# Odd-layer parameters gathered into one DRAM array, and the second half's norm placed between projections

## The chip, the cores and the metric

The kernel runs on one core of a Trainium2 chip. A core has five engines: TensorE (PE; its weight loads are shown apart as PEld), VectorE (DVE), ScalarE (ACT), GpSimd (POOL) and SyncE (SP). Each runs its own instructions strictly in order and waits on semaphores for the others. SP computes nothing here; it issues nearly all loads and stores between DRAM and the on-chip memory (SBUF), which 16 DMA engines then carry out from queues. The metric is the device time of one execution in microseconds.

## The reference, cut to what matters

A trunk of two layers works on x, 1024 tokens by 1024 features, in float32. Layer 0 (even) has an S5 state-space model and stick-breaking attention side by side; layer 1 (odd) has RWKV-7 and Mamba-2 side by side. Each mixer is followed by a mixture of experts (32 experts, two per token). Every sub-layer is normed and modulated by shift, scale and gate vectors that a matrix ada_w makes of the conditioning vector c:

```python
def odd_mixer(h, w_in, w_out, rw_mu, rw_w0, rw_w2, rw_a0, rw_a2, rw_g2, rw_k_k, rw_k_a,
              rw_r_k, rw_ln_w, rw_ln_b, m2_conv_w, m2_conv_b, m2_dt_bias, m2_a_log, m2_d, m2_norm_w):
    proj = h @ w_in
    y_c = rwkv7_mixer(proj[..., :RW_IN], rw_mu, rw_w0, rw_w2, rw_a0, rw_a2, rw_g2,
                      rw_k_k, rw_k_a, rw_r_k, rw_ln_w, rw_ln_b)
    y_d = mamba2_mixer(proj[..., RW_IN:], m2_conv_w, m2_conv_b, m2_dt_bias, m2_a_log, m2_d, m2_norm_w)
    return jnp.concatenate([y_c, y_d], axis=-1) @ w_out
```

The small vectors and matrices after w_out are the parameters of the odd layer that the change is about: vectors of 512 to 1792 values, a convolution of 4 x 1024, two matrices of 64 x 512 and one of 128 x 512, and an eight-column slice of w_in. What they hold doesn't depend on x.

## The kernel before

Tokens are worked on in eight tiles of 128; the odd layer's first projections run over the first four (the first half), and the second four are normed beside them and put away in DRAM. A float32 product is three matmuls on a high and a low part of each operand: mm3 (L240 to L242). The parts come from split (L136 to L139), ScalarE copying the high part, VectorE subtracting to get the low one, for weights (wh, wl) and for the normed activations (hTh, hTl).

ada (L142) makes the modulation vectors: four pieces of ada_w, 1 MB each, are loaded through SP (wload, L77), VectorE multiplies each by c in eight steps (L160 once, L167 seven times) into adacc, TensorE sums over partitions (L179) and VectorE adds a bias (L180). The first two vectors, scale and shift of the even mixer, need eight pieces and stay in SBUF; later ones are made between other work and stored to mod_d in DRAM (L187), value by value. In the even layer a loop over eight loads of its input weights (L2047) runs the projections. Inside the experts' routing a table tab_d goes to DRAM value by value, too (L1202); u_d, an S5 operand, goes in pieces of 256 bytes (L262).

The odd layer (odd, L1829) begins with norm_S over tiles 0 to 3, then odd_setup, then norm_S over tiles 4 to 7, and only then starts the generator project(0, 13) and runs it dry with poke(1e9) (L1886). poke(us) advances the generator in self.bg until it has reported so many microseconds of work. Norming a tile first completes the experts of layer 0 for it: get loads the residual cx and the two expert outputs cy (L990, L994), VectorE merges them (L1008), for some tiles with POOL (L1005), the result is stored to xm_d (L1854), normed (L131, L201), transposed by TensorE (L106) and modulated (L223 on ScalarE, L225 on VectorE). A projection's result goes through a token shift (L1402) or through m_conv (L1370), a convolution whose part on ScalarE is L1382.

odd_setup (L1216) loads the parameters through SP into a tile each: seven vectors and rk as columns of 128 (col, L111; each value is a piece of four bytes, since neighbours in DRAM lie in different partitions), cw in four (L1260), wdt (L1262), wa2 in two (L1264, L1265), g2 (L1267), dtb and al (L1270, L1272), md (row, L117), and the layer-norm vectors in four (L1308). VectorE then scales some (L1276).

What is written here is not the final order on an engine: the framework's scheduler simulates the program by its own costs and gives each engine an order, in which an instruction may be put ahead of others that stand earlier in the code. In the trace before, the transposes of tiles 4 to 7 already stand between projection matmuls.

Of the kernel before, what the change touches and what calls it, by code (L numbers as in the profile page):

```python
# [23 lines left out]
KD = D // 128  # L24
# [12 lines left out]
class Core:  # L37
# [1177 lines left out]

    def odd_setup(self, one, tag):  # L1216
# [41 lines left out]
        R["cw"] = one.tile([128, 4, 8], FT, name="cw")  # L1258
        for j in range(4):
            nc.sync.dma_start(R["cw"][:, j, :], a["m2_conv_w"][0, j].rearrange("(k p) -> p k", p=128))  # L1260
        R["wdt"] = one.tile([128, KD, 8], FT, name="wdt")
        nc.sync.dma_start(R["wdt"], a["odd_w_in"][0][:, 3328:3336].rearrange("(k p) n -> p k n", p=128))  # L1262
        R["wa2"] = one.tile([128, 512], FT, name="wa2")
        nc.sync.dma_start(R["wa2"][0:64, :], a["rw_w2"][0])  # L1264
        nc.sync.dma_start(R["wa2"][64:128, :], a["rw_a2"][0])  # L1265
        R["g2"] = one.tile([128, 512], FT, name="g2w")
        nc.sync.dma_start(R["g2"], a["rw_g2"][0])  # L1267
# [5 lines left out]
        R["md"] = self.row(one, a["m2_d"][0], "md", 8, nc.sync)  # L1273
# [29 lines left out]

        for nm in ("rw_ln_w", "rw_ln_b"):
            t = R[nm] = one.tile([128, 4, 64], FT, name=nm)
            src = a[nm][0]
            for r in range(2):
                nc.sync.dma_start(t[64 * r:64 * r + 64], bass.AP(tensor=src.tensor, offset=src.offset + 64 * r,  # L1308
                                                                   ap=[[0, 64], [128, 4], [1, 64]]))
# [519 lines left out]
    def odd(self, get, y_d, o, after):  # L1829
# [3 lines left out]
        with ctx:  # L1833
# [17 lines left out]
            with tc.tile_pool(name="nr1", bufs=1) as np_:  # L1851
# [16 lines left out]
            pos = [0]  # L1868

            def project(n0, n1):  # L1870
                for n in range(n0, n1):
                    pos[0] = n
                    h, (_, do, c) = plan[n]
                    load(n + 1)
                    src = box.pop(n)
                    for z in range(2):
                        w = [pj.tile([128, KD, 128], FR, name=x, bufs=2) for x in ("wh", "wl")]
                        self.split(*w, src[:, :, 128 * z:128 * z + 128])
                        yield from do(h, c + z, w, hs, R, pj)
                    pos[0] = n + 1  # L1880
                    if n in (5, 20):
                        yield from self.m_dt(h, hs, R, pj)
# [96 lines left out]
    def even(self, x_src):  # L1979
# [9 lines left out]
        with self.banks("pse", b=4, a=1, d=1, e=2):  # L1989
# [16 lines left out]
            with tc.tile_pool(name="hT", bufs=1, side="right") as hp, tc.tile_pool(name="wsp", bufs=1, side="right") as wp:  # L2006
# [40 lines left out]
                for n in range(8):  # L2047
# [137 lines left out]
```

## Time and profile before

| | us |
|---|---|
| median of 3 runs | 3070.61 |
| lowest, highest | 3070.59, 3075.35 |
| profiled execution | 3069.93 |
| its span (first to last instruction) | 3068.1 |
| TensorE busy | 2656.4 |
| VectorE busy | 1792.6 |
| ScalarE busy | 1120.7 |
| GpSimd busy | 831.2 |

The mean granted TensorE clock was 0.902 of full speed. Busy times are sums over the whole span; they overlap. An engine that is idle matters only where another waits for it in turn, so a table like this tells which engine is busy, and the timelines below tell where it isn't.

### The profile page before, as it was taken

What the parts mean: (1) busy time and instruction counts of PE and PEld (TensorE: products, weight loads), DVE (VectorE), ACT (ScalarE), POOL (GpSimd) and SP (SyncE); (2) the same over time, 40 slices, a digit from 0 to 9 for tenths busy, and PEclk for the clock granted to TensorE, in tenths of its full rate; (3) what the DMA queues carried; (4) which work ended last, traced back from release to release, by engine and by line L of the source; (5) the groups of instructions that cost most, each with busy time, mean ns of one, the idle gap of its engine ahead of it and who ended that gap; (6) DMA issues with size and microseconds to landing.
All of it is one profiled execution on the core that took longest, in us unless ns stands there. A gap on an engine that the chain in (4) does not pass through costs nothing. (4 is left out here: it accounts for less than half of the span.)

```text
span 3068.1 us, 39923 instructions
## 1 busy us (share of the span) xinstructions
PE 2656.4 (87%) x14357; PEld 1854.7 (60%) x14357; DVE 1792.6 (58%) x3211; ACT 1120.7 (37%) x1777; POOL 831.2 (27%) x1157
## 2 busy tenths in 40 slices
PE   4987688989699999995799999999978799998991
PEld 4776466647444466662677777777877444566660
DVE  7546999655633477664734555646547434556664
ACT  4311456432232345552433323323233223345451
POOL 5260755324211031101301533354105111111101
PEclk9998689989799999997898978886988799999996
DMA  8746220223588899997745322244443689999995
GB/s 279 178 124 198 63 59 15 90 68 105 211 338 324 351 368 407 376 389 256 260 138 176 110 77 78 67 121 103 107 125 119 242 348 365 369 362 396 388 385 239
DMA packets 345018, 672.82 MB, mean 219 GB/s; under 512 B 118591, under 2 KB 259935, under 8 KB 293104
## 3 DMA queue, kind: packets, MB, share of 16 engines
q1 hardware_dynamic: 272960, 611.23, 54.7%
q10 hardware_dynamic: 56752, 25.41, 3.0%
q0 software_dynamic: 15104, 33.58, 3.0%
q8 instruction: 115, 1.88, 0.3%
q14 instruction: 87, 0.71, 0.1%
HBM read 611.31 MB, written 79.79 MB: 225 GB/s over the span
## 5 line engine op out<-in xcount | busy, mean ns | idle before, releaser
L139 DVE TENSOR_TENSOR wlo<-w,whi 128x1024 fp32r<-128x1024 f32 x384 | 451.4, 1220 | 114.0 <-ACT whi L138 112.3
L138 ACT ACTIVATE whi<-w 128x1024 fp32r<-128x1024 f32 x384 | 390.5, 1054 | 237.1 <-PE ps_g L839 69.9
L240 PE MATMUL ps_b<-hTh,wh 128*128 128x512 f32 x608 | 259.3, 428 | 28.2 <-ACT cc L1382 12.5
L241 PE MATMUL ps_b<-hTl,wh 128*128 128x512 f32 x608 | 255.2, 420 | 0.0
L242 PE MATMUL ps_b<-hTh,wl 128*128 128x512 f32 x608 | 254.8, 419 | 0.0
L788 POOL DMA_INDIRECT xg<-h_d,tok x56 | 80.6, 1440 | 641.6 <-PE ps_t L106 617.1
L847 DVE TENSOR_TENSOR hs<-hs,ps_u 128x512 f32<-128x512 f32 x48 | 32.9, 685 | 263.3 <-PE ps_u L917 212.4
L794 POOL DMA_INDIRECT ye_d<-y,tab x48 | 71.9, 1497 | 421.8 <-DVE y L856 328.4
L167 DVE SCALAR_TENSOR_TENSOR adacc<-w,cs,adacc 128x256 f32<-128x256 f32 x329 | 161.1, 507 | 5.2
L139 DVE TENSOR_TENSOR wl<-w,wh 128x1024 fp32r<-128x1024 f32 x84 | 104.0, 1253 | 97.3 <-ACT wh L138 88.1
L240 PEld LDWEIGHTS ps_b<-hTh,wh 128*128 128x128 f32 x608 | 124.8, 206 | 55.9 <-ACT cc L1382 13.3
L846 ACT ACTIVATE hs<-ps_g 128x512 f32<-128x512 f32 x48 | 28.7, 598 | 325.0 <-PE ps_g L917 244.8
L313 DVE TENSOR_TENSOR_SCAN sP<-keep,sP,sbz 128x256 f32<-128x256 f32 (+1 forms) x160 | 132.9, 874 | 21.7 <-POOL keep L307 10.5
L917 PE MATMUL ps_g<-w,xh 128*64 128x512 f32 x512 | 143.5, 598 | 0.0
L133 POOL TENSOR_TENSOR rs<-rm,nhalf 128x1 f32<-128x1 f32 (+2 forms) x56 | 49.9, 892 | 344.9 <-DVE rm L131 293.2
L138 ACT ACTIVATE wh<-w 128x1024 fp32r<-128x1024 f32 x84 | 86.3, 1053 | 150.5 <-PE ps_b L241 132.4
L241 PEld LDWEIGHTS ps_b<-hTl,wh 128*128 128x128 f32 x608 | 124.7, 205 | 27.2 <-DVE hTl L139 0.3
L242 PEld LDWEIGHTS ps_b<-hTh,wl 128*128 128x128 f32 x608 | 123.9, 204 | 28.3 <-issue 0.4
L917 PE MATMUL ps_u<-w,xh 128*64 128x512 f32 x512 | 137.6, 595 | 0.0
L315 POOL TENSOR_TENSOR sw<-sw,sP 128x512 f32<-128x512 f32 (+1 forms) x80 | 101.1, 1265 | 132.6 <-DVE sP L313 57.3
L926 PE MATMUL ps_y<-w,hh 128*64 128x512 f32 x512 | 122.0, 598 | 2.2 <-ACT hh L921 2.2
L1699 POOL TENSOR_TENSOR T<-N,X 128x60 f32<-128x60 f32 (+24 forms) x248 | 87.1, 351 | 125.2 <-DMA N<-n_d 93.3
(709 smaller groups left out, 6177.9 us busy)
## 6 DMA issues: line engine op xcount, KB each, us to landing
w<-in_moe_w_gate_dram SPq DMA_DIRECT2D x128, 1024.0 KB, 14.7
w<-in_moe_w_up_dram SPq DMA_DIRECT2D x128, 1024.0 KB, 14.8
w<-in_moe_w_down_dram SPq DMA_DIRECT2D x128, 1024.0 KB, 13.4
w<-in_ada_w_dram SPq DMA_DIRECT2D x48, 1024.0 KB, 5.8
w<-in_odd_w_in_dram SPq DMA_DIRECT2D x26, 1024.0 KB, 5.7
cy<-ye_d SPq DMA_DIRECT2D x16, 1024.0 KB, 10.8
cx<-xm_d SPq DMA_DIRECT2D x29, 512.0 KB, 7.5
w<-in_even_w_in_dram SPq DMA_DIRECT2D x8, 1024.0 KB, 8.5
```

The lines of the kernel that those rows point to most:

```text
L138: self.nc.scalar.activation(hi, x, AF.Copy)
L139: self.nc.vector.tensor_tensor(lo, x, hi.bitcast(FT), op=OP.subtract)
L167: eng.scalar_tensor_tensor(acc, wk, ck, acc, op0=OP.mult, op1=OP.add)
L240: nc.tensor.matmul(p, a[0], b[0], start=first, stop=False)
L241: nc.tensor.matmul(p, a[0], b[1], start=False, stop=False)
L242: nc.tensor.matmul(p, a[1], b[0], start=False, stop=last)
L313: v.tensor_tensor_scan(P[:, r, 0:n][:, ::-1], keep[:, r, 0:n][:, ::-1], zero.to_broadcast([128, n]), P[:, r, n:n + 1], op0=OP.mult, op1=OP ...
L315: g.tensor_tensor(w[:, :, 0:n], w[:, :, 0:n], P[:, :, 1:n + 1], op=OP.mult)
L788: nc.gpsimd.indirect_dma_start(out=xg, out_offset=None, in_=h_d[:], in_offset=bass.IndirectOffsetOnAxis(ap=tokc, axis=0), bounds_check=T - ...
L917: nc.tensor.matmul(ps[z][r], x[:, 4 * h + k, r], w[z][h][:, k, :], start=(h == 0 and k == 0), stop=(h == 1 and k == 3))
L926: nc.tensor.matmul(py[n][r], ht[:, f, r], w[2][f // 2][:, f % 2, two[n]], start=(f == 0), stop=(f == 3))
L1699: g.tensor_tensor(o, N[:, 0:j, j:j + 1].to_broadcast([128, j, w]), X[:, j:j + 1, c:8].to_broadcast([128, j, w]), op=OP.mult)
```

## The change

Three edits. First, a new function pack, called in the even layer's loop at its seventh weight load, copies 15 parameters of the odd layer from DRAM to DRAM, into one array pk_d of 128 rows by 1686 values, laid out as SBUF wants them; odd_setup then loads pk_d by one transfer into the tile pk and uses slices of it (dtb and al are still loaded by themselves). Second, norm_S of tiles 4 to 7 is called in two pairs, each after poke(18) of the projection generator, which is created before. Third, the two steps on al (Exp and the sign) stand right behind odd_setup.

```diff
+    def pack(self):
+        nc, a = self.nc, self.a
+        self.pk, parts, c = {}, [], 0
+        col = lambda src: src.rearrange("(k p) -> p k", p=128)
+        for nm, n in (("rw_w0", 4), ("rw_a0", 4), ("rw_k_k", 4), ("rw_k_a", 4), ("m2_conv_b", 8), ("m2_norm_w", 4), ("rw_mu", 14)):
+            parts.append((nm, n, [(slice(0, 128), slice(0, n), col(a[nm][0]))]))
+        parts.append(("rk", 4, [(slice(0, 128), slice(0, 4), col(a["rw_r_k"][0].rearrange("h n -> (h n)")))]))
+        parts.append(("cw", 32, [(slice(0, 128), slice(8 * j, 8 * j + 8), col(a["m2_conv_w"][0, j])) for j in range(4)]))
+        wdt = a["odd_w_in"][0][:, 3328:3336].rearrange("(k p) n -> p k n", p=128)
+        parts.append(("wdt", 64, [(slice(0, 128), slice(8 * k, 8 * k + 8), wdt[:, k]) for k in range(KD)]))
+        parts.append(("wa2", 512, [(slice(0, 64), slice(0, 512), a["rw_w2"][0]), (slice(64, 128), slice(0, 512), a["rw_a2"][0])]))
+        parts.append(("g2", 512, [(slice(0, 128), slice(0, 512), a["rw_g2"][0])]))
+        md = a["m2_d"][0]
+        parts.append(("md", 8, [(slice(0, 128), slice(0, 8), bass.AP(tensor=md.tensor, offset=md.offset, ap=[[0, 128], [1, 8]]))]))
+        for nm in ("rw_ln_w", "rw_ln_b"):
+            src = a[nm][0]
+            parts.append((nm, 256, [(slice(64 * r, 64 * r + 64), slice(64 * h, 64 * h + 64),
+                                     bass.AP(tensor=src.tensor, offset=src.offset + 128 * h + 64 * r, ap=[[0, 64], [1, 64]]))
+                                    for r in range(2) for h in range(4)]))
+        self.pk_n = sum(n for _, n, _ in parts)
+        self.pk_d = self.dram.tile([128, self.pk_n], FT, name="pk_d")
+        for nm, n, pieces in parts:
+            self.pk[nm] = c, n
+            for rows, cols, src in pieces:
+                nc.sync.dma_start(self.pk_d[rows, c + cols.start:c + cols.stop], src)
+            c += n
...
-        for nm, n in (("rw_w0", 4), ("rw_a0", 4), ("rw_k_k", 4), ("rw_k_a", 4),
-                      ("m2_conv_b", 8), ("m2_norm_w", 4), ("rw_mu", 14)):
-            R[nm] = self.col(one, a[nm][0], nm, n, nc.sync)
-        R["rk"] = self.col(one, a["rw_r_k"][0].rearrange("h n -> (h n)"), "rkc", 4, nc.sync)
+        pk = one.tile([128, self.pk_n], FT, name="pk")
+        nc.sync.dma_start(pk, self.pk_d[:])
+        for nm, (c, n) in self.pk.items():
+            R[nm] = pk[:, c:c + n]
...
-        for j in range(4):
-            nc.sync.dma_start(R["cw"][:, j, :], a["m2_conv_w"][0, j].rearrange("(k p) -> p k", p=128))
...
-        nc.sync.dma_start(R["g2"], a["rw_g2"][0])
...
-                for h, d in enumerate((hs, ht)):
-                    if h == 1:
-                        R = self.odd_setup(one, "a")
-                    self.norm_S(getx, self.mod["scale1", 1], self.mod["shift1", 1], *d, np_, "tk", range(4 * h, 4 * h + 4))
+                mod = self.mod["scale1", 1], self.mod["shift1", 1]
+                self.norm_S(getx, *mod, *hs, np_, "tk", range(4))
+                R = self.odd_setup(one, "a")
+                nc.scalar.activation(R["al"], R["al"], AF.Exp)
+                nc.vector.tensor_scalar(R["al"], R["al"], -1.0, None, op0=OP.mult)
...
+                self.bg = [project(0, 13)]
+
+                for t in (4, 6):
+                    self.poke(18)
+                    self.norm_S(getx, *mod, *ht, np_, "tk", range(t, t + 2), 128 * (t - 4))
...
-            nc.scalar.activation(R["al"], R["al"], AF.Exp)
-            nc.vector.tensor_scalar(R["al"], R["al"], -1.0, None, op0=OP.mult)
-            self.turn_tag = "t"
-            self.bg = [project(0, 13)]
             self.poke(1e9)
...
+                    if n == 6:
+                        self.pack()
```

Where the new transfers come to stand is the scheduler's doing. On SP at the very start of the program, before (xt is a tile of x, w a piece of a weight matrix; xN counts equal neighbours):

```order
L2013 DMA xt<-in_x_dram 128x1024 x4
L77 DMA w<-in_ada_w_dram 128x8x256 x4
L2013 DMA xt<-in_x_dram 128x1024 x2
L77 DMA w<-in_ada_w_dram 128x8x256
L2013 DMA xt<-in_x_dram 128x1024
L77 DMA w<-in_ada_w_dram 128x8x256
```

And the same place in the changed kernel:

```order
L2030 DMA xt<-in_x_dram 128x1024 x4
L77 DMA w<-in_ada_w_dram 128x8x256 x4
L1241 DMA pk_d<-in_rw_w_dram 128x4x1
L1241 DMA pk_d<-in_rw_a_dram 128x4x1
L1241 DMA pk_d<-in_rw_k_k_dram 128x4x1
L1241 DMA pk_d<-in_rw_k_a_dram 128x4x1
L2030 DMA xt<-in_x_dram 128x1024
L1241 DMA pk_d<-in_m_conv_b_dram 128x8x1
L1241 DMA pk_d<-in_m_norm_w_dram 128x4x1
L1241 DMA pk_d<-in_rw_mu_dram 128x14x1
L1241 DMA pk_d<-in_rw_r_k_dram 128x4x1
L1241 DMA pk_d<-in_m_conv_w_dram 128x8x1 x2
```

Behind these rows come another xt, the last two transfers of conv_w and one of wdt, and then the fifth piece of ada_w. So all transfers with single values in them have moved between the fourth and the fifth piece; the rest of the 40 follow among the pieces five to eight and the first input weights of the even layer.

On SP at the odd layer's start, before, from its second weight load on:

```order
L1264 DMA wa_11386<-in_rw_w_dram 64x512
L1854 DMA xm_d<-cx 128x1024
L1265 DMA wa_11386<-in_rw_a_dram 64x512
L1267 DMA g2w<-in_rw_g_dram 128x512
L1270 DMA dtb<-in_m_dt_bias_dram 8x1
L1272 DMA al<-in_m_a_log_dram 8x1
L117 DMA md<-in_m_d_dram 128x8
L1308 DMA rw_ln_w<-in_rw_ln_w_dram 64x4x64 x2
L1854 DMA xm_d<-cx 128x1024
L1308 DMA rw_ln_b<-in_rw_ln_b_dram 64x4x64 x2
L994 DMA cy<-ye_d 128x2048 x2
L77 DMA w<-in_odd_w_in_dram 128x8x256
```

And in the changed kernel:

```order
L77 DMA w<-in_odd_w_in_dram 128x8x256
L1279 DMA pk<-pk_d 128x1686
L1292 DMA dtb<-in_m_dt_bias_dram 8x1
L1294 DMA al<-in_m_a_log_dram 8x1
L77 DMA w<-in_odd_w_in_dram 128x8x256
L1868 DMA xm_d<-cx 128x1024 x3
L994 DMA cy<-ye_d 128x2048 x2
L1868 DMA xm_d<-cx 128x1024
L77 DMA w<-in_odd_w_in_dram 128x8x256
```

The cy loads now stand behind one parameter load, a second weight load and three stores of x, where before all the single loads stood ahead of them.

On TensorE, the place where transposes of tiles 4 to 7 first stand between the projections' matmuls, before (ps_t and ps_k are the transposes' accumulators, ps_b the projection's):

```order
L240 MATMUL ps_b<-hTh,wh 128x512
L106 MATMUL ps_t<-ident,cy 128x128
L106 MATMUL ps_k<-ident,cy 128x128 x2
L241 MATMUL ps_b<-hTl,wh 128x512
L242 MATMUL ps_b<-hTh,wl 128x512
L240 MATMUL ps_b<-hTh,wh 128x512
L106 MATMUL ps_t<-ident,cy 128x128 x3
L106 MATMUL ps_k<-ident,cy 128x128 x6
```

And after:

```order
L106 MATMUL ps_t<-ident,cy 128x128 x4
L106 MATMUL ps_k<-ident,cy 128x128 x8
```

The first pair's transposes come about six groups of three matmuls later and stand in one bunch of twelve; four more of that pair follow behind further projection matmuls.

## Rows read from the trace of the kernel before

**Rows 1.** The page: span; each engine's busy time; a group of instructions (busy, mean ns).
```profile
span 3068.1 us, 39923 instructions
...
PE 2656.4 (87%) x14357; PEld 1854.7 (60%) x14357; DVE 1792.6 (58%) x3211; ACT 1120.7 (37%) x1777; POOL 831.2 (27%) x1157
...
L167 DVE SCALAR_TENSOR_TENSOR adacc<-w,cs,adacc 128x256 f32<-128x256 f32 x329 | 161.1, 507 | 5.2
```

**Rows 2.** Windows: us, each engine's busy time, granted clock, DMA share, GB/s.
```profile
0.00:20.00 20.00, 4.20 (x16) 3.00 (x16) 6.86 (x20) 8.26 (x14) 12.57 (x13) 1.00 0.95 292
...
15.00:20.00 5.00, 3.51 (x14) 2.71 (x14) 4.82 (x9) 2.39 (x4) 4.90 (x4) 1.00 1.10 372
```

**Rows 3.** Timeline of SP's queue at the start: start, duration, line, transfer, count.
```profile
5.62 8.47 SPq L77 DMA_DIRECT2D w<-in_ada_w_dram  x4
...
20.83 0.38 SPq L77 DMA_DIRECT2D w<-in_ada_w_dram  x1
```

**Rows 4.** Timeline of DVE: first step of ada pieces five, seven, eight; the shift.
```profile
28.58 0.34 DVE L160 TENSOR_SCALAR adacc<-w,cs 128x256 f32<-128x256 f32 x1
...
39.66 1.17 DVE L160 TENSOR_SCALAR adacc<-w,cs 128x256 f32<-128x256 f32 x1
...
44.21 0.35 DVE L160 TENSOR_SCALAR adacc<-w,cs 128x256 f32<-128x256 f32 x1
...
50.86 0.17 DVE L180 TENSOR_TENSOR shift<-ps_e,adac 128x8 f32<-128x8 f32 x1
```

**Rows 5.** Timeline of PE: the first projection matmul [idle before, its releaser].
```profile
60.40 1.22 PE L240 MATMUL ps_b<-hTh,wh 128*128 128x512 f32 x2 [9.58 <-ACT hTh L138]
```

**Rows 6.** Timeline of DVE at the odd layer's start.
```profile
1452.40 0.18 DVE L1276 TENSOR_SCALAR cw<-cw 128x32 f32<-128x32 f32 x1 [1.76 <-DMA cw<-in_m_conv_w_dram]
...
1457.05 0.43 DVE L1276 TENSOR_SCALAR g2w<-g2w 128x512 f32<-128x512 f32 x1 [2.69 <-DMA g2w<-in_rw_g_dram]
...
1472.30 1.29 DVE L1008 SCALAR_TENSOR_TENSOR cx<-cy,gates,cx 128x1024 f32<-128x1024 f32 x1 [7.10 <-issue]
```

**Rows 7.** Timeline of SP's queue at the odd layer's start.
```profile
1428.61 7.21 SPq L111 DMA_DIRECT2D rw_w<-in_rw_w_dram  x1
...
1445.40 1.00 SPq L1854 DMA_DIRECT2D xm_d<-cx  x1
...
1458.43 1.04 SPq L994 DMA_DIRECT2D cy<-ye_d  x2
```

**Rows 8.** Timeline of PE there: first projection, and the third block of them.
```profile
1461.40 1.20 PE L240 MATMUL ps_b<-hTh,wh 128*128 128x512 f32 x2
...
1484.60 0.80 PE L240 MATMUL ps_b<-hTh,wh 128*128 128x512 f32 x1 [10.80 <-ACT cc L1382]
```

**Rows 9.** Waits of PE, 1460 to 1560: total us, times, longest us.
```profile
PE ps_b L240 <- ACT cc L1382: 12.5, 2, 10.8
PE ps_t L106 <- DVE acc L1402: 4.6, 1, 4.6
PE ps_k L106 <- ACT hm L223: 1.3, 1, 1.3
```

**Rows 10.** DMA view, 1442 to 1452 us: all packets, while small parameters load.
```profile
DMA packets 10741, 0.67 MB, mean 67 GB/s; under 512 B 10533, under 2 KB 10612, under 8 KB 10740
```

**Rows 11.** Line L187 (store of mod_d, eight times): issue to landing.
```profile
DMA to landing us min/median/max: 12.0/12.2/12.5
```

**Rows 12.** Window during the fifth such store.
```profile
286.00:297.00 11.00, 3.40 (x14) 2.25 (x14) 3.68 (x14) 1.02 (x1) 4.03 (x6) 0.68 0.48 23
```

**Rows 13.** Timeline of DVE behind it.
```profile
301.47 0.35 DVE L160 TENSOR_SCALAR adacc<-w,cs 128x256 f32<-128x256 f32 x1 [11.58 <-DMA w<-in_ada_w_dram]
```

**Rows 14.** Line L1202 (store of tab_d): issue to landing.
```profile
DMA to landing us min/median/max: 36.2/37.3/38.5
```

**Rows 15.** DMA view, 1107 to 1116 us: packets of the queue with that store.
```profile
q10 hardware_dynamic: 2290, 0.01, 16.2%
```

**Rows 16.** Line L262 (store of u_d, 256-byte pieces): issue to landing.
```profile
DMA to landing us min/median/max: 3.0/3.1/11.4
```

More of the change, by code (lines that the diff above doesn't have):

```diff
@@ L1249, in odd_setup @@
         v.tensor_copy(hbk[:].rearrange("p h k -> p (h k)"), ph[0:8])
-        for nm, n in (("rw_w0", 4), ("rw_a0", 4), ("rw_k_k", 4), ("rw_k_a", 4),
-                      ("m2_conv_b", 8), ("m2_norm_w", 4), ("rw_mu", 14)):
-            R[nm] = self.col(one, a[nm][0], nm, n, nc.sync)
-        R["rk"] = self.col(one, a["rw_r_k"][0].rearrange("h n -> (h n)"), "rkc", 4, nc.sync)
+        pk = one.tile([128, self.pk_n], FT, name="pk")
+        nc.sync.dma_start(pk, self.pk_d[:])
+        for nm, (c, n) in self.pk.items():
+            R[nm] = pk[:, c:c + n]
+        R["cw"] = R["cw"].rearrange("p (j k) -> p j k", j=4)
+        R["wdt"] = R["wdt"].rearrange("p (k n) -> p k n", k=KD)
+        for nm in ("rw_ln_w", "rw_ln_b"):
+            R[nm] = R[nm].rearrange("p (h d) -> p h d", h=4)
         R["nkk"] = one.tile([128, 4], FT, name="nkk")
@@ L1257, in odd_setup @@
         v.tensor_scalar(R["omu"], R["rw_mu"], -1.0, 1.0, op0=OP.mult, op1=OP.add)
-        R["cw"] = one.tile([128, 4, 8], FT, name="cw")
-        for j in range(4):
-            nc.sync.dma_start(R["cw"][:, j, :], a["m2_conv_w"][0, j].rearrange("(k p) -> p k", p=128))
[L1261 to L1266, printed above, removed]
-        nc.sync.dma_start(R["g2"], a["rw_g2"][0])
         R["dtb"] = one.tile([8, 1], FT, name="dtb")
@@ L1272, in odd_setup @@
         nc.sync.dma_start(R["al"], a["m2_a_log"][0].rearrange("(h o) -> h o", o=1))
-        R["md"] = self.row(one, a["m2_d"][0], "md", 8, nc.sync)
         for x in ("rw_w0", "rw_a0", "rw_k_a", "m2_conv_b", "cw", "g2"):
@@ L1302, in odd_setup @@
         v.tensor_scalar(bd[:, 0:1], R["odd32"], -1.0, 1.0, op0=OP.mult, op1=OP.add)
[L1304 to L1309, printed above, removed]
         R["n_d"] = self.dram.tile([8, 32, 1024], FT, name="n_d")
@@ L1860, in odd, with project @@
                 load(0)
-                for h, d in enumerate((hs, ht)):
-                    if h == 1:
-                        R = self.odd_setup(one, "a")
-                    self.norm_S(getx, self.mod["scale1", 1], self.mod["shift1", 1], *d, np_, "tk", range(4 * h, 4 * h + 4))
+                mod = self.mod["scale1", 1], self.mod["shift1", 1]
[3 more added lines that the diff above has]
+                nc.vector.tensor_scalar(R["al"], R["al"], -1.0, None, op0=OP.mult)
+                pos = [0]
+                def project(n0, n1):
+                    for n in range(n0, n1):
+                        pos[0] = n
+                        h, (_, do, c) = plan[n]
+                        load(n + 1)
+                        src = box.pop(n)
+                        for z in range(2):
+                            w = [pj.tile([128, KD, 128], FR, name=x, bufs=2) for x in ("wh", "wl")]
+                            self.split(*w, src[:, :, 128 * z:128 * z + 128])
+                            yield from do(h, c + z, w, hs, R, pj)
+                        pos[0] = n + 1
+                        if n in (5, 20):
+                            yield from self.m_dt(h, hs, R, pj)
+                self.turn_tag = "t"
+                self.bg = [project(0, 13)]
+                for t in (4, 6):
+                    self.poke(18)
+                    self.norm_S(getx, *mod, *ht, np_, "tk", range(t, t + 2), 128 * (t - 4))
                 h_d = self.dram.tile([2, 128, KD * 512], FT, name="h_d")
@@ L1867, in odd @@
                     nc.scalar.dma_start(h_d[z], ht[z][:].rearrange("p k t -> p (k t)").bitcast(FT))
[L1868 to L1882, printed above, removed]
-            nc.scalar.activation(R["al"], R["al"], AF.Exp)
-            nc.vector.tensor_scalar(R["al"], R["al"], -1.0, None, op0=OP.mult)
-            self.turn_tag = "t"
-            self.bg = [project(0, 13)]
             self.poke(1e9)
```

## The prediction

> **What bounds the kernel now.** The page comes first: the span is 3068.1 us and TensorE is busy for 2656.4 us of it, VectorE for 1792.6 [rows 1]. The profiled execution took 3069.93 us, 1.83 over its span, and lies 0.68 under the median of the runs shown; the sum below is made against 3069.93. An average of 87% says that TensorE sets the pace in most stages, not in which it waits. So I looked at the two places that the change touches, the start (the gather) and the first projections of the odd layer, by windows, then by each engine's timeline.
>
> At the start the core waits for loads. In the first 20 us the DMA engines are 95% busy at 292 GB/s and TensorE works 4.20 us [rows 2]. SP has put four pieces of ada_w into its queue by 14.1 us, behind four x tiles; the fifth piece follows at 20.83 [rows 3]. VectorE multiplies each piece as it comes: the fifth from 28.58 us, the seventh and eighth from 39.66 and 44.21, so 4.55 us a piece, and the finished shift stands at 50.86 [rows 4]. The first matmul of a projection comes at 60.40 us, after 9.58 us of waiting for the normed tile [rows 5]. What makes the fifth piece late makes this late, and no TensorE work lies beside it.
>
> In the odd layer VectorE waits 1.76 us for cw and 2.69 us for g2w, and later stands 7.10 us before the merge of expert outputs at 1472.30 [rows 6]. The view names "issue"; SP's queue shows the true releaser: the cy loads of that merge are issued at 1458.43 only, behind the parameter loads, the first of them at 1428.61 [rows 7]. Instructions of one engine run in order, so the convolution steps queued behind that merge wait too, and TensorE, whose projections begin at 1461.40, stands 10.80 us until 1484.60 for them [rows 8]. Smaller waits follow up to 1560: 1.7 more of the 12.5 on the convolution, 4.6 for a shift step and 1.3 for a modulation, 18.4 in all with the 10.80 [rows 9].
>
> **The gather's cost.** pack() issues 40 transfers from DRAM to DRAM on SP. 78 columns of 128 values go element by element, 9984 pieces of 4 bytes. Wdt adds 1024 pieces of 32 bytes and md 128, the layer-norm vectors 1024 of 256 bytes, and three matrices 0.5 MB in rows of 2 KB. The code calls it in the even layer's loop, but the scheduler puts the first 13 transfers between the fourth and the fifth load of ada_w, so all 9984 elements stand in the queue ahead of the piece that VectorE needs at 28.58.
>
> No such transfer is in the trace; bounds come from its neighbours.
> - Lowest: the same parameters loaded into SBUF, 10533 small packets within a window of 10 us [rows 10]. So C = 10 us.
> - Highest: the store of mod_d writes 1024 four-byte elements to DRAM and lands after 12.2 us [rows 11]; in 11 us of it the loads run at 23 GB/s only, and VectorE then waits 11.58 us for a piece of ada_w [rows 12, 13]. That is 11 us / 1024 = 10.7 ns each, C = 9984 x 10.7 ns = 107 us.
> - Between: the store of tab_d, 4096 such elements, lands after 37.3 us [rows 14], but beside weight loads; its last 2290 passed in at most 9 us as those ended [rows 15]. That is 3.9 ns each, C = 39 us.
>
> I take 39: tab_d writes neighbouring words of one row from one partition, as the gather does, while mod_d strides.
>
> The Trainium skill, "DMA: Bandwidth & Descriptors", section "Specifications", says that a transfer under 512 bytes makes the DMA read, modify and write. By that all 12160 pieces under 512 bytes would cost alike, 12160 x 3.9 ns = 47 us, and the sum would be 8 us higher, 3107. Stores of u_d, 1024 pieces of 256 bytes, mostly land in 3.1 us [rows 16], which speaks against one price for all; I keep it for four-byte writes.
>
> Ahead of the fifth piece stand four x tiles and four pieces, 6.29 MB. 5.84 MB are through at 20 us (292 GB/s x 20), the rest by about 21. Then come C and 2.1 MB (two x tiles and the fifth piece), 5.6 us at the 372 GB/s of the last 5 of those 20 us [rows 2]. So the piece lands at 21 + 39 + 5.6 = 65.6, against 28.58: 37 us late. The rest of the gather lies mostly between pieces five and eight: 1024 small pieces x 3.9 ns = 4.0 us, 0.5 MB about 1.4, four of the wide transfers, half of u_d's 1024, about 1.5 by half its 3.1 us. The three loads are 2.8 us each against 4.55 of VectorE work, which takes back 5. So D = 37 + 7 - 5 = 39 us of delay for all that follows. With C = 10, D is 21 + 10 + 5.6 - 28.6 = 8 and the rest is hidden; with C = 107 the small pieces cost 11 us too, and D = 105 + 14 - 5 = 114.
>
> **What the odd layer gains.** 21 small loads of parameters give way to one of 863 KB (128 x 1686 x 4 bytes), issued behind one weight load; at 372 GB/s that is 2.3 us, so it lands before VectorE asks. The waits of 1.76 and 2.69 go, 4.45 us ahead of the first projection. VectorE's scalings stay, 0.18 us for cw and 0.43 for g2w [rows 6]. Three stores of x stay ahead of the cy loads; the first was issued at 1445.40 amid the parameters [rows 7], so cy can come up to 13 us earlier than 1458.43, and with half of that the 7.10 us that VectorE stood for it are nearly gone. Norming moves behind two stretches of projections, but it was woven between the matmuls before as well, as TensorE's order shows; in the new order the transposes come later and in bunches of 12, and what is late next is the modulation of the normed tiles, 1.3 us at the longest [rows 9]. Of 4.45 + 7.10 = 11.55 I take G = 10. The ends: 4.4, if the waits behind the merge only move, and 4.4 + 18.4 = 23, if every wait of [rows 9] goes as well. Moving the two steps on al costs nothing: 8 x 1 elements behind the load.
>
> **The even layer's order.** The scheduler reshuffles it a little: when the S5 scan begins, 20 fewer multiply steps of ada are done, 507 ns each [rows 1], so up to 10 us more for VectorE there; against that the 11.58 us wait [rows 13] may vanish. I take 0, with -12 to +10.
>
> **Sum.** 3069.93 + 39 - 10 + 0 = 3099 us.
>
> **The rivals.** The profile can tell 0.2%, 6 us, from no change.
> - *A. Cheap gather.* Four-byte stores cost like the loads of [rows 10]: 3069.93 + 8 - 10 = 3068, no change. For it: both move as many elements. Against: both stores of such elements to DRAM are slower [rows 11, 14]. In a sentence of its own: the Trainium skill, same page, "Why small descriptors are slow (HBM only)", puts the price in a fixed overhead of each packet and its descriptor, which reading and writing would share; the trace bears that out for loads, not for these stores. Chance 0.17.
> - *B. Faster.* The gather is cheap and the order frees the odd layer's start: with cy in time and the second half's norm spread, the waits on the convolution and the shift go too. 3069.93 + 8 - 23 = 3055. It decides where D is under G - 6, which with G = 23 is a gather under about 19 us. For it: all those waits have VectorE, which is relieved, as the releaser or behind it. Against: D as above. Chance 0.18.
> - *C. Dear gather.* Every element pays mod_d's price: 3069.93 + 114 - 10 = 3174. For it: loads almost stop beside mod_d [rows 12]. Against: tab_d's last part [rows 15]. Chance 0.15.
> - *D. The second part does not do what it says.* Norming was interleaved before, so only the parameters' 4.4 are won: 3069.93 + 39 - 4.4 = 3105. Chance 0.05.
>
> **How the numbers follow.** The forecast has 0.45, with 3080 to 3130 as its own range (C from about 22 to 67). Slower is forecast, C and D, 0.65; same is A, 0.17; faster is B, 0.18. The range for 8 in 10 goes from just under B's 3055 to just over C's 3174: 3053 to 3180.
>
> **What would show it.** In the changed kernel: a stretch from about 21 to 60 us with DMA busy but few GB/s, VectorE's fifth piece at about 65 instead of 28.58, the first projection matmul at about 100 instead of 60.40, and from there a constant lag until the odd layer. There: no wait for cw or g2w, cy issued right behind the parameters' load, no 10.80 us hole of TensorE, and the lag about 10 us smaller by 1560. The forecast is wrong if the fifth piece comes before 45 us (A or B), if the lag at the first projection is over 80 (C), or if the even layer absorbs the lag because VectorE, not TensorE, sets its end and can use the idle time.

## The result and the profile after

The changed kernel took 3153.99 us (median of 4; 3145.11 to 3160.81) against 3071.23 for the kernel before: ratio 1.0265, 95% interval 1.0246 to 1.0284, 83 us slower. The forecast was 29 us slower (39 - 10). The profiled execution of the changed kernel took 3157.94 us, 88 more than that of before.

To see where these went, each TensorE instruction of the changed kernel was matched to the same one of the kernel before (engine, source text, tiles, and the count of its kind), and the median difference of their starts taken by stretch. This lag is worked out from the two traces. It is sharp where both kernels have the same order; between 1600 and 2300 the orders differ, and at 1900 the median moves by some 5 us with the width of the stretch:

| us of before | lag, us | what lies between |
|---|---|---|
| 60 (first projection) | +46.9 | the gather at the start: +47 |
| 700 (end of the even mixer) | +60.8 | the even layer: +14 |
| 1400 (end of its experts) | +66.0 | +5 |
| 1600 (odd projections) | +54.7 | the odd layer's start: -11 |
| 1900 | +46.0 | recurrences, first part: -9 |
| 2300 | +82.6 | recurrences, second part: +37 |
| 2950 | +87.5 | second experts: +5 |

The page of the changed kernel, first its span and engine totals (to be read beside [rows 1]):

```profile
span 3156.2 us, 39933 instructions
...
PE 2680.1 (85%) x14357; PEld 1866.9 (59%) x14357; DVE 1789.0 (57%) x3213; ACT 1121.2 (36%) x1775; POOL 806.7 (26%) x1157
```

VectorE does 4 us less work and TensorE shows 24 us more, at a mean granted clock of 0.895 instead of 0.902; the rest is waiting. The clock is a part of the 88: the changed kernel's fastest run, at 0.902 like the profiled execution of before, took 3145.11 us, 75 more than that.

**The start.** SP's queue in the changed kernel (start, duration, line, transfer), which answers to [rows 3]; the last row is the fifth piece of ada_w:

```profile
14.22 3.48 SPq L1241 DMA_DIRECT2D pk_d<-in_rw_w_dram  x1
...
24.05 4.61 SPq L1241 DMA_DIRECT2D pk_d<-in_rw_mu_dram  x1
...
46.78 8.95 SPq L1241 DMA_DIRECT2D pk_d<-in_odd_w_in_dram  x1
55.84 0.54 SPq L77 DMA_DIRECT2D w<-in_ada_w_dram  x1
```

The DMA view of the changed kernel from 22 to 55 us, all packets, and the window of the same stretch (columns as in [rows 2]):

```profile
DMA packets 8165, 1.12 MB, mean 34 GB/s; under 512 B 7873, under 2 KB 7909, under 8 KB 8165
```
```profile
22.00:55.00 33.00, 10.16 (x47) 9.86 (x46) 5.26 (x12) 1.15 (x2) 3.59 (x2) 1.00 0.69 34
```

7873 small pieces in 33 us are 4.2 ns each (the prediction took 3.9). The queue moves 34 GB/s where before it moved 292 to 372, and the DMA engines count as 69% busy: a busy share without bytes is the sign of small pieces. VectorE's timeline, answering to [rows 4], and TensorE's first projection, to [rows 5]:

```profile
68.63 0.35 DVE L160 TENSOR_SCALAR adacc<-w,cs 128x256 f32<-128x256 f32 x1 [11.37 <-DMA w<-in_ada_w_dram]
...
83.33 0.15 DVE L131 TENSOR_SCALAR rm<-ss 128x1 f32<-128x1 f32 x1 [8.91 <-ACT xn L124]
87.26 0.35 DVE L160 TENSOR_SCALAR adacc<-w,cs 128x256 f32<-128x256 f32 x1
91.39 0.35 DVE L160 TENSOR_SCALAR adacc<-w,cs 128x256 f32<-128x256 f32 x1
...
97.83 0.16 DVE L180 TENSOR_TENSOR shift<-ps_e,adac 128x8 f32<-128x8 f32 x1
```
```profile
106.48 1.22 PE L240 MATMUL ps_b<-hTh,wh 128*128 128x512 f32 x2 [9.77 <-ACT hTh L138]
```

The fifth piece is 40 us late (68.63 against 28.58), the eighth, in the fourth row, 47. The 7 between them stand in the second row: in the middle of its steps of ada VectorE waits 8.91 us for the norm of an x tile on ScalarE (L124). ScalarE's timeline tells why that is late:

```profile
81.17 0.38 ACTq L111 DMA_DIRECT2D adac<-in_ada_b_dram  x1
81.59 0.60 ACT L213 ACTIVATE qT<-ps_a 128x512 f32<-128x512 f32 x1 [23.62 <-DMA pk_d<-in_m_d_dram]
82.08 1.05 ACT L124 ACTIVATE xn<-xt 128x1024 f32<-128x1024 f32 x1
```

ScalarE reads nothing of pk_d. But in its order the small load of a bias, which it issues itself, stands ahead of L213, and the program gives all its transfers eight landing semaphores in turn (DMAHW0 to DMAHW7); a transfer waits until the last user of its semaphore has landed. For this load that was a transfer of the gather on SP's queue: the trace has the last landing on DMAHW5 at 81.1 us and the load's issue at 81.17. In the order of the changed kernel, with the semaphores waited for:

```
L111 DMA adac<-in_ada_b_dram 128x8x1 [waits DMAHW5_49,DMAHW1_49,DVE_49]
L213 ACTIVATE qT<-ps_a 128x2x256 [waits PE_49]
```

**The even layer.** A wait of VectorE that the kernel before hasn't got:

```profile
195.94 3.19 DVE L139 TENSOR_TENSOR wl<-w,wh 128x1024 fp32r<-128x1024 f32 x2 [19.65 <-ACT wh L138]
```

The high part on ScalarE comes no later than the general lag (194.84 us against 147.85), but steps of ada that VectorE did meanwhile before now stand behind this split and wait with it. When the split starts, 123 steps (L160 and L167) are done, where before had done 148; 25 steps at 507 ns [rows 1] are 12.7 us. They are missing in the stretch of 300 to 540 us, which VectorE bounds: before it was busy for 232.79 of those 240 us. VectorE's waits between the first projection and 700 us of before, first before, then after, say the same (total us, times, longest us):

```profile
DVE adacc L160 <- DMA w<-in_ada_w_dram: 69.4, 20, 11.6
...
DVE wl L139 <- ACT wh L138: 1.3, 2, 0.7
```
```profile
DVE adacc L160 <- DMA w<-in_ada_w_dram: 62.6, 15, 14.3
DVE wl L139 <- ACT wh L138: 21.0, 3, 19.6
```

The waits for high parts grow by 19.7 us, those for pieces of ada_w shrink by 6.8: 13 us, near the 14 of the lag.

**The odd layer's start.** SP and TensorE there, answering to [rows 7] and [rows 8], and TensorE's waits from 1515 to 1615, to [rows 9]:

```profile
1495.97 7.42 SPq L1279 DMA_DIRECT2D pk<-pk_d  x1
...
1511.06 2.35 SPq L994 DMA_DIRECT2D cy<-ye_d  x2
```
```profile
1523.41 1.20 PE L240 MATMUL ps_b<-hTh,wh 128*128 128x512 f32 x2
...
1542.65 0.79 PE L240 MATMUL ps_b<-hTh,wh 128*128 128x512 f32 x1 [6.83 <-ACT cc L1396]
```
```profile
PE ps_b L240 <- ACT cc L1396: 10.7, 4, 6.8
PE ps_t L106 <- DVE acc L1416: 3.7, 1, 3.7
PE ps_k L106 <- DVE hm L225: 3.4, 2, 3.2
```

The first projection is 62.0 us later than before, the third block 58.1, where the lag was 66.0 just ahead: 4.0 won by the first, 4.0 more by the third, 11 by 1600. No wait for cw or g2w is left. The hole of 10.80 is 6.83 wide now, not gone.

**The recurrences.** From 1650 us of before on, the odd layer's projections stand between the steps of its recurrences, chains in which each step needs the one before. To see where the time goes, count steps: RWKV's chain has 16, each with 16 of the trace's matmul records at L1760 (L1774 after), in the same sequence in every kernel here. For the first twelve steps the changed kernel takes 431.7 us and the kernel before 436.3, so nothing is lost yet. The last four take 116.4 us instead of 83.5. As windows of these four, before and after:

```profile
2088.00:2172.00 84.00, 75.83 (x703) 61.93 (x702) 45.87 (x92) 25.30 (x71) 29.02 (x69) 0.75 0.39 100
```
```profile
2138.50:2255.00 116.50, 92.14 (x836) 78.32 (x836) 56.80 (x116) 35.56 (x97) 35.38 (x81) 0.73 0.42 105
```

TensorE works 16 us more there (148 output matmuls, ps_o from yT, are done in it instead of 64) and is idle for 16 us more, longest for UV and C, two steps of RWKV on VectorE (10.5 us in two waits, 7.4 in one). What follows, up to 2350 us of before, takes 178 us in both kernels, although the changed one has less left to do: TensorE waits in it for om, VectorE's step on a finished output block, 15.9 us instead of 4.5, before and after:

```profile
PE ps_o L681 <- DVE om L684: 4.5, 2, 2.3
```
```profile
PE ps_o L681 <- DVE om L684: 15.9, 3, 7.2
```

The worst 50 us of the changed kernel:

```profile
2150.00:2200.00 50.00, 33.03 (x279) 26.36 (x280) 22.55 (x51) 17.68 (x48) 17.30 (x41) 0.65 0.36 104
```

TensorE is busy 33 of 50 us, and no other engine is over 23: no engine is the bound, the chains are.

The lag's fall to 46 by 1900 is no gain. The odd layer has 1296 records of projection matmuls (ps_b from hTh or hTl), which fill the gaps between steps of the chain. At the start of the seventh step the changed kernel is only 14 us late (1922.6 against 1908.5 us), but with 978 of the 1296 done, where before had done 1075. The lead of the chain is filler put off, and by the thirteenth step, where both have done all 1296, it is used up.

The clock has a part in this, too. From 1600 to 2350 us of before TensorE is busy for 691.8 us at a mean granted clock of 0.85; in the changed kernel the same work takes 704.3 at 0.83, so 12.5 of the 28 us are TensorE's own. Whether the idle time brought the lower clock or the lower clock the longer work isn't shown. That the clock alone moves this stretch little, one run suggests, the last of those below: with every computing engine in the order of before, TensorE was busy for 681.8 us at 0.86, 10 less than before, and the stretch was only 3 us shorter.

### The profile page after: what moved, and what is told of

Its sections match the earlier page's. It is cut to its first block, busy times and chain, and to the rows that moved or that the text cites. A ratio compares the mean times of both kernels' runs of the same rounds, so it can differ in the third digit from the quotient of the medians.

```text
span 3156.2 us, 39933 instructions
## 1 busy us (share of the span) xinstructions
PE 2680.1 (85%) x14357; PEld 1866.9 (59%) x14357; DVE 1789.0 (57%) x3213; ACT 1121.2 (36%) x1775; POOL 806.7 (26%) x1157
## 5 line engine op out<-in xcount | busy, mean ns | idle before, releaser
L240 PE MATMUL ps_b<-hTh,wh 128*128 128x512 f32 x608 | 260.9, 431 | 27.3 <-ACT cc L1396 10.7
L167 DVE SCALAR_TENSOR_TENSOR adacc<-w,cs,adacc 128x256 f32<-128x256 f32 x329 | 168.3, 527 | 5.1
L313 DVE TENSOR_TENSOR_SCAN sP<-keep,sP,sbz 128x256 f32<-128x256 f32 (+1 forms) x160 | 127.8, 840 | 23.9 <-POOL keep L307 11.6
```

What stands on the lines that cost most here:

```text
L167: eng.scalar_tensor_tensor(acc, wk, ck, acc, op0=OP.mult, op1=OP.add)
L240: nc.tensor.matmul(p, a[0], b[0], start=first, stop=False)
L313: v.tensor_tensor_scan(P[:, r, 0:n][:, ::-1], keep[:, r, 0:n][:, ::-1], zero.to_broadcast([128, n]), P[:, r, n:n + 1], op0=OP.mult, op1=OP ...
```

## The experiments

Each was run beside the kernel before on the same chip, and ratios are to that. Lags are to the one trace of before, so each has a few us of its run's own: the eight kernels that keep before's order in the even layer, and have no gather there, stand at -2 to +8 at 700 us, and from 1600 to 2400 the lag went by +10 and by -5 in the two that have before's order there (the first edit alone, the layer-norm loads moved). The four with the largest lags of their own (norm alone, first edit alone, SBUF tile, rows) were run where the kernel before took 3082.56 us. Traced executions lie up to 10 us off their medians: the contiguous gather's took 3128.37 (median 3120.63), that of cw in one transfer 3065.18 (3060.69), that with the layer-norm loads moved 3060.74 (3071.23).

**Each edit by itself.** Only the second and third edit (loads as in the kernel before):

```diff
+                self.norm_S(getx, *mod, *hs, np_, "tk", range(4))
+                R = self.odd_setup(one, "a")
...
+                for t in (4, 6):
+                    self.poke(18)
+                    self.norm_S(getx, *mod, *ht, np_, "tk", range(t, t + 2), 128 * (t - 4))
```

> Only the second edit: the parameters are loaded one by one as before, norm_S of tiles 4 to 7 is called between the projections, the steps on al come earlier. Each engine's order up to the odd layer is that of the kernel before, so the first projection matmul should stand at 60.4 us and the lag against before should be 0 (within 2 us) up to 1400 us in both theories. Theory 1 (the 88 us of the change are three things: about 46 at the start from the gather's four-byte writes to DRAM, about 19 in the even layer and its experts from a new order there, and about 28 in the odd layer after 1700 us from a new order there): the waits for cw and g2w stay (4.45 us), the odd layer's order after 1700 us is new again, so the time is 3071 within about 30, by luck of that order. Theory 2 (the interleaved norm itself makes the odd layer's second part slower): 28 us slower after 1700 us, about 3095.

Ratio 1.0047 (1.0024 to 1.007). Lag -0.5 at the first projection; 3 won at the odd layer's start; between 1600 and 1900 the lag falls by 15, then rises by 28. The early part costs nothing beyond that (7.9 at 700 us), the late part does, with no gather in the kernel.

Only the first edit (pack and the single load; norm_S and al as before):

```diff
+                    if n == 6:
+                        self.pack()
...
+        pk = one.tile([128, self.pk_n], FT, name="pk")
+        nc.sync.dma_start(pk, self.pk_d[:])
```

> Only the first edit: gather and single load, norm_S and al as before. Up to the odd layer each engine's order is that of the changed kernel, in the odd layer's second part nearly that of the kernel before. Theory 1 (order): first projection at 106 us, lag of 61 to 66 us at 1400 us, about 10 us won at the odd layer's start, no further loss between 1700 and 2250 us: about 3071 + 66 - 10 = 3127, a few us more behind it. Theory 2 (parameters as slices of one tile, or the clock, make the odd layer slower whatever the order): the lag grows from 55 to 83 us there as in the changed kernel, about 3155.

Ratio 1.0207 (1.0184 to 1.0231), 63 us. Lag 52 at the first projection, 69 at 700, VectorE again in the long wait:

```profile
202.79 2.75 DVE L139 TENSOR_TENSOR wl<-w,wh 128x1024 fp32r<-128x1024 f32 x2 [19.13 <-ACT wh L138]
```

11 won at the odd layer's start, without the interleaved norm: that gain belongs to the single load. After 1600, in the order of before, it loses 9, not 28: theory 2 of that expectation falls, for its parameters are slices of the same tile. With poke(9) in place of poke(18) the full change, as built, has exactly this kernel's order on every engine (it was not run), so what the second edit moved, at 18, is little more than the order of the recurrences.

**What the start pays for.** The same transfers at the same place, landing in SBUF, then one store in rows of 568 bytes:

```diff
+        pb = self.const.tile([128, 142], FT, name="pb")
...
+                dst = pb if c < 142 else self.pk_d
+                nc.sync.dma_start(dst[rows, c + cols.start:c + cols.stop], src)
...
+                nc.sync.dma_start(self.pk_d[:, 0:142], pb)
```

> The changed kernel, but the 9984 four-byte pieces and the 1024 of 32 bytes of wdt are gathered into a tile in SBUF (the same transfers at the same place in SP's queue) and stored from there into pk_d in rows of 568 bytes. Theory 1 (four-byte writes to DRAM are the price): the fifth piece of ada_w is used at about 28.6 + 8 to 12 us instead of 68.6, first projection at about 70, and, as the order of the even layer is nearly the same as in the changed kernel, 14 us are still lost between the first projection and the first experts: 3154 less 36 = 3118 with the same luck in the odd layer, 3090 with better. Theory 3 (the number of transfers or of pieces in front of the fifth piece is the price, wherever they land): fifth piece at about 68 as before, about 3154.

VectorE's fifth piece and TensorE's first projection:

```profile
39.39 0.35 DVE L160 TENSOR_SCALAR adacc<-w,cs 128x256 f32<-128x256 f32 x1 [4.23 <-DMA w<-in_ada_w_dram]
```
```profile
78.77 1.22 PE L240 MATMUL ps_b<-hTh,wh 128*128 128x512 f32 x2 [10.08 <-ACT hTh L138]
```

10.8 us late instead of 40, as expected; the projection 18.4 instead of 46.1, since ScalarE still waits, 17.14 us, for a transfer into pk_d. So 28 us of the start are the writes of small pieces (9984 of four bytes, 1024 of 32) to DRAM instead of SBUF. The ratio is 1.0243 (1.0225 to 1.026), little better than the change: from the first projection to 700 us the lag grows by 22, some 7 of which the chip has of its own (6 and 8 in the two kernels without a gather run beside it), and after 1600 it loses 38. VectorE's long wait is there, too:

```profile
169.93 2.91 DVE L139 TENSOR_TENSOR wl<-w,wh 128x1024 fp32r<-128x1024 f32 x2 [19.65 <-ACT wh L138]
```

A gather of contiguous pieces at the same place (rows of an array of 78 x 128; the odd layer transposes them once on TensorE):

```diff
+                if c < 78:
+                    nc.sync.dma_start(self.pr_d[o, :], src.rearrange("p k -> k p"))
...
+        self.transpose(ph[:, 0:78], pr, 78)
+        v.tensor_copy(pk[:, 0:78], ph[:, 0:78])
```

> The changed kernel with a gather of the same number of transfers at the same place in SP's queue, but the 78 columns are copied as rows, in contiguous pieces, into an array of 78 x 128 in DRAM; the odd layer loads it as such and TensorE transposes it once. The scheduler's order of the even layer is then that of the kernel before (98 to 100% alike on every engine but SP), not that of the changed one. If the price of the start is the four-byte writes: the fifth piece under 8 us late, first projection at 65 to 72 us. If the 14 us between there and the first experts come from the order: none of them here, the lag stays at that of the first projection, and VectorE's wait of 19.65 us for a weight's high part is gone; if they come from the gather's transfers in SP's queue, 14 us again. At the odd layer's start 8 to 11 us won. After 1700 us the order is that of the run with the gather through SBUF, which lost 38 us there: again about 35 if the order alone does it. Sum 3071 + 8 - 10 + 35 = 3104.

```profile
33.15 1.20 DVE L160 TENSOR_SCALAR adacc<-w,cs 128x256 f32<-128x256 f32 x1 [2.55 <-DMA w<-in_ada_w_dram]
```
```profile
70.94 1.22 PE L240 MATMUL ps_b<-hTh,wh 128*128 128x512 f32 x2 [10.64 <-ACT hTh L138]
```

4.6 us late, projection 10.5 late. With the even layer's order of before the wait of 19 us is gone (all waits for high parts come to 3.8 us up to 700, against 19.9 to 21.0 in the three kernels with the other order), and the lag grows by 7 to 700 us, where it grows by 14, 18 and 22 in those three: about half of the even layer's loss is shown to go with its order; what the other 7 are, and how much of them is the run's own, stays open. Ratio 1.0153 (1.0133 to 1.0173), since after 1600 it loses 41 (up to 8 of them this execution's own), in TensorE's and VectorE's order of the kernel with the SBUF tile, which lost 38. Two kernels, two starts, one order, nearly one loss.

The gather held back until v is done (a first transfer from v into pk_d makes it wait):

```diff
-                    if n == 6:
-                        self.pack()
+            self.pack(v)
...
+        nc.sync.dma_start(self.pk_d[:], hold[:].rearrange("p t d -> p (t d)")[:, 0:self.pk_n])
```

> The changed kernel, with the gather held back: pk_d is first written once, by one transfer of 863 KB, from v, which is done at the end of the even layer's projections (about 300 us), so all 40 transfers come behind that. Both theories: fifth piece of ada_w at 28.6 us and first projection at 60.4 us as before, so the 46 us of the start are gone. Theory A (the price of the gather is paid wherever loads stand behind it in SP's queue): VectorE, which multiplies pieces of ada_w all through 300 to 540 us, waits there for 30 to 45 us more than before, and by the first experts the lag is 30 to 45 us; with 10 to 30 us for the new order in the odd layer 3110 to 3145 against a before of 3071. Theory B (it costs only where nothing else is to be done): under 10 us by the first experts, 3080 to 3100.

Ratio 1.0116 (1.008 to 1.0151). Start as before (lag 0.2), then 33 lost by 700, at one place; VectorE's wait, and its sum from 280 to 720 us (before, from 280 to 690: 20.9 in all, the longest 11.6):

```profile
316.55 0.35 DVE L160 TENSOR_SCALAR adacc<-w,cs 128x256 f32<-128x256 f32 x1 [33.12 <-DMA w<-in_ada_w_dram]
```
```profile
DVE adacc L160 <- DMA w<-in_ada_w_dram: 48.3, 4, 33.1
```

Theory A stands: the price moves with the gather to whatever load is queued behind it. From 1600 to 2400 this kernel's order loses nothing (27.0 at both).

**Whether an order alone moves the recurrences.** Four transfers of cw made one, with the same pieces; nothing else:

```diff
-        for j in range(4):
-            nc.sync.dma_start(R["cw"][:, j, :], a["m2_conv_w"][0, j].rearrange("(k p) -> p k", p=128))
+        nc.sync.dma_start(R["cw"][:].rearrange("p j k -> p (j k)"), a["m2_conv_w"][0].rearrange("j (k p) -> p (j k)", p=128))
```

> The kernel before with one thing changed: the four loads of cw are one transfer with the same 4096 pieces. Up to 1430 us no engine's order changes; the scheduler then gives the odd layer after 1700 us another order (32 to 68% alike in slices of TensorE's instructions, against 100% for edits that the scheduler doesn't feel). Theory 1 (order alone moves the odd layer's second part by 10 to 40 us): lag about 0 at 1600 us, and between -10 and +40 by 2300, more likely a loss, since before's is the best of the orders seen: +10 to +20. Theory 2 (the order is worth nothing, and what the interleaved kernels lost there comes from the norm's place): within 4 us of before at 2300.

Ratio 0.9962 (0.9945 to 0.9979; 10 runs, median 3060.69 against 3070.83): faster than both kernels. In the traced execution 3 us are won at the odd layer's start and 10 between 1600 and 2400, of which 8 are lost again by the end. The expected sign was wrong, before's order isn't the best; that an order is worth about 10 us by itself is shown by the ten runs, as the work is the same.

The second edit with 30 us in place of 18:

```diff
-                    self.poke(18)
+                    self.poke(30)
```

> Only the second edit, as in the run of that edit alone, but with 30 us of projections instead of 18 ahead of each pair of tiles; parameters loaded one by one. A second order of the odd layer from the same edit. Theory 1 (luck of the order): up to 1700 us within 5 us of the 18-us version, after it a different amount, anywhere between -5 and +40. Theory 2 (norming later is what costs): more than with 18, which lost about 13 us from 1900 to the end against its before.

Ratio 1.011 (1.0082 to 1.0138): 6 to 10 lost between 1500 and 1600, by the stretch taken, where with 18 us nothing was, and 17 from 1600 to 2300 against 13. This alone doesn't tell the two theories apart; the next group does.

**The small loads by themselves, and more orders.** The columns as 78 rows of 512 bytes, transposed once, no gather:

```diff
+            nc.sync.dma_start(pr[c:c + n, :], src)
+            R[nm] = pc[:, c:c + n]
...
+        self.transpose(ph[:, 0:78], pr, 78)
+        v.tensor_copy(pc, ph[:, 0:78])
```

> The kernel before with one thing changed: the 78 columns of parameters are loaded as 78 rows of 512 bytes into one tile (9 transfers, 78 pieces instead of 9984), which TensorE transposes once; no gather, norm_S as before. Even layer as before, lag 0 up to 1420 us. If the four-byte pieces are what VectorE waits for in the odd layer (1.76 for cw, 2.69 for g2w, and 7.10 for cy behind them): 5 to 11 us won by 1500 us, then the luck of the new order after 1700 us (within 30). If the wait is one on SP's issues of the remaining 12 transfers: under 3 us won by 1500.

Ratio 1.0024 (1.0007 to 1.0042). 8 us won at the odd layer's start, as expected of the pieces, 13 lost after 1600. The same with the copy on ScalarE (`nc.scalar.copy(pc, ph[:, 0:78])`):

> The kernel with the columns loaded as rows and transposed once, with the transposed tile copied by ScalarE instead of VectorE: another order of the odd layer. At the odd layer's start about 8 us won as in that kernel; after 1700 us by the luck of the order -10 to +38: between 3053 and 3100 against 3071, most likely slower than before by about 5.

Ratio 1.0008 (0.9988 to 1.0027), no change: 11 won at the start, 22 more by 1900, and 20 given back by 2300. Rows for cw alone:

```diff
+        pr = one.tile([32, 128], FT, name="pr")
+        nc.sync.dma_start(pr, a["m2_conv_w"][0].rearrange("j (k p) -> (j k) p", p=128))
+        self.transpose(ph[:, 0:32], pr, 32)
```

> Kernel before with cw alone loaded as 32 rows of 512 bytes in one transfer and transposed (4096 of the 9984 small pieces gone); norm and the rest as before. At the odd layer's start 3 to 6 us won (the wait of 1.76 for cw, and cy three issues earlier); after 1700 us another order again, -10 to +38. Between 3055 and 3105.

Ratio 0.9974 (0.9956 to 0.9991). 4 won at the start, 3.5 after. Rows together with the interleaved norm at 30 us:

> Columns loaded as rows and transposed once, and the second half normed in pairs behind 30 us of projections: another order of the odd layer. 8 us won at its start, then -10 to +38 after 1700 us by its order; if norming later costs of itself, the loss is above 20 as in the other kernels with 18 and 30 us (23 and 27 between 1600 and 2300).

Ratio 1.0011 (1.0000 to 1.0022): 9 won by 1500 and, with the norm this late, 10 lost by 1600 again, as in the other kernel with 30 us; but after 1600 it loses 1, where that lost 17. So the loss in the recurrences isn't the late norm's; it goes with the order. A last one moved the layer-norm loads behind the first projections:

```diff
             self.poke(1e9)
+            for nm in ("rw_ln_w", "rw_ln_b"):
+                t = R[nm] = one.tile([128, 4, 64], FT, name=nm)
```

> The kernel before with the four loads of the layer-norm vectors called after the first projections instead of in odd_setup; the order of TensorE and VectorE is that of the kernel before throughout. The cy loads then stand 3 to 4 us earlier in SP's queue. If VectorE's 7.10 us at 1472 are a wait for cy behind the parameter loads: 3 to 4 us won by 1490, kept to the end if nothing else is late next: 3067 against 3071. If POOL's or another step ends the wait: under 1 us.

Ratio 1.0005 (0.9994 to 1.0017). The scheduler called three of the four up again, cy was issued at 1455.84 with all else 3.3 us early on that chip, so it moved by nothing, and the run says nothing on the wait for cy. With the order of every computing engine that of before, its lag of -6.4 at 2300 shows what a chip and a single profile can have of their own.

In these eleven kernels, with ten orders of the recurrences, those that run ahead until 1900 give it back by 2300, most of them more than it. Change of lag, 1600 to 1900 and 1900 to 2300, in us: the change -9, +37; norm alone -15, +28; SBUF tile -15, +54; contiguous gather -14, +55; 30 us -15, +32; copy on ScalarE -22, +20; held -12, +12; rows -2, +15; rows and 30 us -2, +3; cw in one transfer +4, -14; rows for cw +6, -10. The values at 1900 are good to some 5 us, the sum of the two to the spread of -5 to +10 given above: the losses of 17 and more are clear of it, those of 13 hardly. Counted as above, the seven kernels that lead by 9 us or more at 1900 have done 978 to 1020 of the 1296 projection matmuls when the seventh step of RWKV's chain begins, the other four 1056 to 1094, and the kernel before 1075: in all of them the early lead goes with filler put off. Their last four steps take 104 to 119 us, where before took 84; but so do those of the two kernels that load all columns as rows and copy them on VectorE, which lost 13 and 1, so this alone doesn't set the loss. That an order moves the time is shown; which of its waits is to blame is not, for no run changes one of them by itself.

## Why the prediction was right in sign and wrong in size

- **C, the gather's four-byte writes:** right in size. 4.2 ns each against 3.9, the fifth piece at 68.63 us against 65.6. The reason given for taking tab_d's price and not mod_d's, neighbouring words, was tested by no run, so the choice between them may be luck. That the price is the landing in DRAM, and that it falls on what is queued behind, the SBUF tile and the held gather show. In the Trainium skill, "DMA: Bandwidth & Descriptors", section "Specifications" has one rule for everything under 512 bytes; the trace does not bear out one price: the same four-byte pieces cost 29 us less when they land in SBUF.
- **D, the delay of all that follows:** mis-sized, 47 against 39. The piece itself was 40 late against 37; the sum followed VectorE's pieces alone. It missed ScalarE, which waits 23.62 us for a transfer of the gather it doesn't use, through a landing semaphore in common, and holds VectorE by 8.91 us.
- **The even layer's order, taken as 0 with -12 to +10:** failed. It lost 14. The prediction saw that steps of ada move, up to 10 us of them, and set that off against a wait for ada_w that might vanish. 25 steps moved (12.7 us), the waits for ada_w shrank by 6.8 us only, and the move made a wait that it hadn't looked for: a split of a weight, now ahead of the steps, waits 19.65 us for ScalarE. In the kernel that has the gather's transfers and before's order there, that wait is gone and the loss is 7.
- **G, the odd layer's start, 10:** right, 11, of it 4.0 before the first projection (forecast 4.45). The reason for the rest was right in part: cy comes earlier, but the hole of TensorE narrows to 6.83 instead of closing, and rival D was right that the interleaved norm moves hardly anything there.
- **No term for the recurrences:** the step that failed most. The sum put all that lies after 1560 at nothing, without a reason. The edit gave the scheduler other starting times and it reordered 600 us of work: 28 us by 2300, 33 by the end with the experts. With the first edit alone, which keeps before's order there, the same stretch lost 9. The sizes: 47 + 14 + 5 - 11 + 28 + 5 = 88.

The time lies inside the range for 8 in 10 (3053 to 3180), but outside the forecast's own, 3080 to 3130. It lies nearer to rival C's than to the forecast's, but not for C's reason: the elements didn't pay mod_d's price.

## What to carry to other kernels

Data that is wanted early must not stand behind a rearrangement in the same queue: write such a rearrangement as contiguous pieces and turn it on TensorE, which left 10.5 us of the start's 46, or let it land in SBUF, which left 18; the four-byte pieces into DRAM cost 4.2 ns each here, to everything behind them. Where a scheduler sets the order, compare the whole order of every engine after an edit, not only the place of the edit: merging four loads into one was worth -10 us with the same work, and one order that two kernels share cost them 38 and 41. A stretch that gains early because its filler is put off has to be followed to its end before the gain is counted.

## What the runs showed of the hardware

- Four-byte pieces from DRAM to DRAM pass at 4.2 ns each (7873 in 33 us), with the DMA engines 69% busy at 34 GB/s; the same pieces into SBUF delayed the load behind them by 10.8 us instead of 40 (10512 pieces under 512 bytes passed in the 14 us from 22 on, so 1.3 ns each).
- mod_d's 1024 four-byte stores had gone at 10.7 ns each [rows 11, 12]. Why these are dearer isn't known from these runs.
- An engine can wait for a transfer that it has nothing to do with: 23.62, 24.36, 17.14 and 13.15 us on ScalarE in the four kernels with the gather at the start (the change, the first edit alone, the SBUF tile, the contiguous gather), for the transfer that held the landing semaphore in turn.
